# Gate projections of a hybrid layer, started ahead of the recurrence

## The chip, the cores and the metric

The kernel runs on one core of a Trainium2 chip. The metric is the device time of one execution in microseconds; the median of three runs is compared. The profile is of one more execution.

## The reference, cut to what matters

Two layers work on 256 context rows and 1024 latent rows of width 1024. Each layer norms and modulates the rows to h, projects h, runs three branches (gated linear attention, grouped-query attention, an RWKV-7 recurrence) and merges them:

```python
g1, g2, g3 = split(h @ w_in[:, MERGE], 3)              # merge gates, 3 x 1024 columns
m = (sigmoid(g1) * (ya @ w_o_gla) + sigmoid(g2) * (yb @ w_o_att)
     + sigmoid(g3) * (yc @ w_o_rwkv))
x = x + gate * rms_norm(m @ w_out, g_post)
```

The recurrence of the RWKV branch is a scan over time, forwards and backwards:

```python
sa = einsum('bhvk,bhk->bhv', s, kk_t)
s = s * w_t - sa * (kk_t * a_t) + v_t * k_t
y_t = einsum('bhvk,bhk->bhv', s, r_t)
```

The merge gates need only h. They are needed at the merge, after all branches. The last layer needs no gates for the context rows.

## The kernel before

All tokens are in blocks of 256 (context), 512 and 512 columns (`BLK`); tiles have 128 tokens. A product of full accuracy is three matmuls: each operand is split into a high and a low part (`split`, one ACT copy and one DVE subtraction), and high x high, high x low and low x high are summed in PSUM.

A layer has these stages: projections, gated linear attention woven with the attention's projections, the RWKV projections (`rwkv_proj`), then two stages that the change touches, and the merge.

*Attention with the operands.* `rwkv_pre()` makes the operands of the recurrence (decay, key and value factors in `uscr`, the output's factors `gR` and `bR`), block by block and in four groups of 128 rows, and stores them in DRAM. It works on ACT, DVE and POOL and needs little of TensorE; its sums go to the "a" banks of PSUM. `attention()` runs beside it as filler: scores in "mm" banks, transposes in "t", outputs in "o" and "u".

*The pass.* `rwkv()` runs the recurrence: 20 half-steps `q` of 64 tokens in both directions at once. For each, `elem` loads operands and makes AR and BK, `gram` makes products of them and sends a triangular block through DRAM twice (Ms to nscr, back as Lm, 15 steps of DVE, acc to tscr, back as DT and Dg), `merge` builds T from that, and `chain` advances the state S. `merge_gates()` runs beside it as filler: for each block and each of 24 column tiles it loads two times 256 KB of weights (wr), splits them, does 24 matmuls (8 steps of three), and stores the tanh of half the sum to `tg` in DRAM. It begins with the last block, whose normed rows are still in SBUF as `hb[-1]`.

What sets the order: `weave(main, fill, ratio)` takes a step of the main generator, adds `ratio` times its stated length to a debt, and takes steps of the filler until the debt is paid. Steps yield their length: a gate step n / 784, an attention piece n / 256. The program order that comes out is then reordered by the framework's planner (`schedule_with_timeline_sim=True`): for each engine it picks by program order among what it estimates to be ready, and fixes one instruction order for each engine before the run. In the pass the filler has `lead=(0, 8)`: a filler matmul may not be placed before the last matmul of the main step eight steps back. All DMAs are issued on one queue, SP's.

Memory is in pools that open and close like a stack from both sides of SBUF. A new tile waits for the old tiles at its address. On the right, the pool of `merge_gates` comes where `qpool`, the pool of `rwkv_pre`, was. On the left, the pools of the recurrence (`rpool`, `rlate`) come where attention's `bpool` was. `banks(...)` sets which PSUM banks `dense()` hands out in turn: "a", "a" from the RWKV projections' end until the pass, then "mm", "mm", "o". There are two "a" banks.

Of the kernel before, what the change touches and what calls it, by code (L numbers as in the profile page):

```python
# [9 lines left out]
F32 = mybir.dt.float32  # L10
F32R = mybir.dt.float32r
AF = mybir.ActivationFunctionType
# [5 lines left out]
D = 1024  # L18
# [5 lines left out]
BLK = [(0, 256), (256, 512), (768, 512)]  # L24
LAT = [(256, 512), (768, 512)]
GLA0, ATT0, RW0, MG0 = 0, 1568, 3104, 5408
# [44 lines left out]
def hybrid_kernel(ctx: ExitStack, tc: tile.TileContext, I: dict, C: dict, out: bass.AP):  # L71
    nc = tc.nc
    dma = nc.sync.dma_start
    act = nc.scalar.activation
# [18 lines left out]
    pe = PE  # L93

    def nm(s):
        cnt[0] += 1
        return f"{s}{cnt[0]}"
# [3 lines left out]
    def popen(**kw):  # L101
        g = tc.tile_pool(bufs=1, reuse_waits="tile", **kw)
        open_pools.append(g)
        return g, g.__enter__()

    def pclose(g):
        open_pools.remove(g)
        g.__exit__(None, None, None)
# [8 lines left out]
    def ps(tag):  # L117
        return psp.tile([128, 512], F32, tag=tag, bufs=PSB[tag], name=nm("ps_" + tag))
# [3 lines left out]
    def banks(*tags):  # L122

        ring["tags"], ring["i"] = tags, 0

    def dense():
        ring["i"] += 1
        return ps(ring["tags"][(ring["i"] - 1) % len(ring["tags"])])
# [18 lines left out]
    for j in range(2):  # L147
        vec.tensor_scalar(
            out=sil[:, :, j, :], in0=cth[:, j, :].unsqueeze(2).to_broadcast([128, 8, 16]),
# [11 lines left out]
    def dt(name, shape):  # L161
        return dram.tile(shape, F32, name=name)

    yT = {b: dt("yT" + b, [512, NT]) for b in ("att", "gla", "rwkv")}
    tg = [dt(f"tg{i}", [D, NT]) for i in range(3)]
# [4 lines left out]
    xs, hscr = dt("xs", [NT, D]), dt("hscr", [D, NT])  # L170
# [32 lines left out]
    def weave(main, fill, ratio, lead=None, hp=None, to_end=True):  # L203


        due, marks = 0.0, []
        while True:
            with tc.high_priority(offset=hp) if hp else nullcontext():
                w = next(main, None)
            if w is None:  # L210
                break
            marks.append(PE.last.ins)
            due += ratio * (w or 0.0)
            while due > 0.0:
                with tc.issue_after(marks[-1 - lead[1]]) if lead is not None and len(marks) > lead[0] + lead[1] else nullcontext():
                    due -= next(fill, due) or 0.0
        if to_end:
            for _ in fill:
                pass
# [75 lines left out]
    def block_of(b):  # L295

        last = b == len(BLK) - 1
        return [(hX if last else hm).tile([128, 2, BLK[b][1]], F32R, tag=f"b{b}k{k}", name=nm("h")) for k in range(8)]

    def blocks_of(blocks):  # L300
        return [block_of(b) if BLK[b] in blocks else None for b in range(len(BLK))]
# [7 lines left out]
    hb = blocks_of(BLK)  # L309
# [29 lines left out]
    for l in range(DEPTH):  # L339
        need_ctx = l < DEPTH - 1  # L340
        blks = BLK if need_ctx else LAT
# [5 lines left out]
        def split(src, hi, lo):  # L347
            act(out=hi, in_=src, func=AF.Copy)  # L348
            vec.tensor_tensor(out=lo, in0=src, in1=hi.bitcast(F32), op=ALU.subtract)  # L349
# [71 lines left out]
        if l + 1 < DEPTH:  # L421
            mpool, mp = popen(name=nm("modp"))
            md, _ = modulation(l + 1, mp, 2)
# [83 lines left out]
        gpool, gp_ = popen(name=nm("gp"))  # L507
# [324 lines left out]
        def attention():  # L832
# [11 lines left out]
            for g in range(2):  # L844
                kH, kL, V = load(g)
                for t in tiles:
# [56 lines left out]
                    act(out=yo, in_=po[:, :256], func=AF.Copy, scale=0.5)  # L903
                    dma(out=yT["att"][256 * g:256 * g + 256, 128 * t:128 * t + 128].rearrange("(h p) n -> p h n", p=128), in_=yo.rearrange("p (h n) -> p h n", h=2))

        banks("mm", "mm")
        rw = rwkv_proj()
        for _ in range(6):
# [4 lines left out]
        att = attention()  # L913
# [2 lines left out]
        pclose(tpool)  # L916
        pclose(wpool)
        pclose(hpool)
        qpool, qp = popen(name=nm("qp"), side="right")
        weave(rwkv_pre(), att, 4.4)  # L920
        pclose(qpool)
        pclose(bpool)
        rpool, rp = popen(name=nm("rp"))
        def rload(key, shape, src=None):
            t_ = rp.tile(shape, F32, name=nm(key))
            dma(out=t_, in_=C[key] if src is None else src)
            return t_
# [273 lines left out]
        def rwkv():  # L1201
            nq = 2 * NTILE
            es, os = {}, {}

            def put(d, key, steps):
                d[key] = yield from steps

            for w in spread([
                (put(es, 0, elem(0)), 0.0, 0.2, 3.6 + 4 * 2.0),
                (put(os, 0, gram(0, es, 0)), 0.25, 0.5, 5.0 + 6 * 2.0),  # L1210
                (put(os, 1, gram(1, es, 0)), 0.4, 0.65, 5.0 + 6 * 2.0),
                (put(es, 1, elem(1)), 0.6, 0.8, 3.6 + 4 * 2.0),
                (merge(os, 0), 0.75, 1.0, 3.3 + 4 * 2.0),
            ]):
                yield 2.5 * w
            for q in range(nq):
                ths = [(chain(q, os.pop(q)), 0.0, 1.0, 8.3 + 6 * 2.0 + 8 * 2.0 if q % 2 else 8.3 + 6 * 2.0)]
                if q + 1 < nq:
                    ths.append((merge(os, q + 1), *((0.4, 0.9), (0.65, 1.0))[q % 2], 3.3 + 4 * 2.0))
                if q + 2 < nq:  # L1220
                    ths.append((put(os, q + 2, gram(q + 2, es, (q + 2) // 2)), *((0.55, 0.9), (0.1, 0.5))[q % 2], 5.0 + 6 * 2.0))
                if q % 2 == 0 and q // 2 + 1 < NTILE and q:
                    ths.append((put(es, q // 2 + 1, elem(q // 2 + 1)), *(0.0, 0.45), 3.6 + 4 * 2.0))
                yield from spread(ths)


        def merge_gates():
            gpool, gp_ = popen(name=nm("tg"), side="right")
            for t0, n in blks[-1:] + blks[:-1]:
                if (t0, n) == BLK[-1]:  # L1230
                    hx = hb[-1]
                else:
                    hx = block_of(len(BLK) - 1)
                    for k in range(8):
                        raw = gp_.tile([128, 512], F32, tag="wr", bufs=4, name=nm("wr"))[:, :n]
                        dma(out=raw, in_=hscr[128 * k:128 * k + 128, t0:t0 + n])
                        split(raw, hx[k][:, 0, :n], hx[k][:, 1, :n])
                    yield 4.0
                for i in range(3):
                    for m in range(8):  # L1240
                        wh = gp_.tile([128, 8, 128], F32R, tag="wh", bufs=2, name=nm("wh"))
                        wl = gp_.tile([128, 8, 128], F32R, tag="wl", bufs=2, name=nm("wl"))
                        c0 = MG0 + D * i + 128 * m
                        for k in range(0, 8, 4):
                            raw = gp_.tile([128, 512], F32, tag="wr", bufs=4, name=nm("wr")).rearrange("p (k m) -> p k m", k=4)
                            dma(out=raw, in_=I["w_in"][l, 128 * k:128 * k + 512, c0:c0 + 128].rearrange("(k p) m -> p k m", p=128))
                            split(raw, wh[:, k:k + 4], wl[:, k:k + 4])
                        p = dense()[:, :n]
                        for k in range(8):
                            pe.matmul(p, wh[:, k], hx[k][:, 0, :n], start=k == 0, stop=False)  # L1250
                            pe.matmul(p, wh[:, k], hx[k][:, 1, :n], start=False, stop=False)
                            pe.matmul(p, wl[:, k], hx[k][:, 0, :n], start=False, stop=k == 7)
                            if k < 7:
                                yield n / 784
                        th = gp_.tile([128, 512], F32, tag="th", bufs=2, name=nm("th"))[:, :n]
                        act(out=th, in_=p, func=AF.Tanh, scale=0.5)
                        dma(out=tg[i][128 * m:128 * m + 128, t0:t0 + n], in_=th)
                        yield n / 784
            pclose(gpool)

        banks("mm", "mm", "o")
        with tc.manual_schedule(engines={nc.tensor.engine}) if False else nullcontext():
            weave(rwkv(), merge_gates(), (0.76, 0.63)[l], (0, 8), None)
        pclose(rlate)
        pclose(ypool)
        pclose(rpool)
# [27 lines left out]
        for bi, wo in enumerate(("w_o_gla", "w_o_att", "w_o_rwkv")):  # L1294
            if bi == 2:
                mb = blocks_of(blks)
            for jj in range(4):
                wh, wl = load_w([I[wo][l, :, 256 * jj:256 * jj + 256]], kt=4)
                for j in range(2):
                    kr = 2 * jj + j  # L1300
                    w = slice(128 * j, 128 * j + 128)
                    for (t0, n) in blks:
                        th = ta.tile([128, 512], F32, tag="th", bufs=4, name=nm("th"))[:, :n]
                        dma(out=th, in_=tg[bi][128 * kr:128 * kr + 128, t0:t0 + n])
                        p = dense()[:, :n]
# [8 lines left out]
                        m = M[jj][:, j, t0:t0 + n]  # L1314
# [11 lines left out]
        for k in range(8):  # L1326
            wt = cp.tile([128, 2, D], F32R, tag="M", bufs=4, name=nm("wo")) if k < 4 else w2.tile([128, 2, D], F32R, name=nm("wo"))
            for g in range(2):
                gc = slice(512 * g, 512 * g + 512)
                if k < 4:  # L1330
                    raw = cp.tile([128, 512], F32, tag="ws", bufs=2, name=nm("ws"))
                else:
                    if g == 0:
                        xr = oo.tile([128, D], F32, tag="x", bufs=5, name=nm("xr"))
                    raw = xr[:, gc]
# [18 lines left out]
        hb = [None] * len(BLK)  # L1354
# [66 lines left out]
```

## Time and profile before

| | |
|---|---|
| median of 3 runs | 3962.02 us (3959.33 to 3962.11) |
| the profiled execution | 3955.01 us |
| its span, first to last instruction | 3953.2 us |
| mean granted clock of TensorE | 0.962 of full |
| matmuls on TensorE | 31928 |

PE is TensorE's matmuls, PEld its weight loads, DVE VectorE, ACT ScalarE, POOL GpSimd, SPq the queue of SyncE that issues the DMAs. Times in the views count from the span's start. In layer 0 attention with the operands lies at 900 to 1106 us and the pass at 1130 to 1860; in layer 1 at 2900 to 3091 and 3091 to 3720.

### The profile page before, as it was taken

How to read it: one execution, taken by the hardware profiler on the slowest of the kernel's cores; microseconds unless marked ns; L12 is line 12 of the kernel's file. 1: busy time of each engine (PE TensorE's matmuls, PEld its weight loads, DVE VectorE, ACT ScalarE, POOL GpSimd, SP SyncE). 2: the span in 40 equal slices, each digit the busy share in tenths (PEclk: the TensorE clock that was granted, in tenths of full speed). 3: DMA queues.
4: the chain of work that ended last, by engine and by line, in shares of the span. 5: the costliest groups of instructions: out<-in, count | busy, mean ns of one | idle time of the engine just before them, and what ended most of it. 6: DMA issues, size and time to landing. Idle time of an engine off the chain costs nothing.

```text
span 3953.2 us, 81725 instructions
## 1 busy us (share of the span) xinstructions
PE 3698.9 (94%) x31928; PEld 3092.6 (78%) x31928; DVE 2100.1 (53%) x5083; ACT 1761.0 (45%) x4099; POOL 604.9 (15%) x714
## 2 busy tenths in 40 slices
PE   4999999999979989999999999999999899999899
PEld 2799887887767778777888899877878677777687
DVE  3234344437865766664453244444378676666562
ACT  3244437437843444344234344365388333343422
POOL 1133230001200000000233142300022000000042
PEclk7999999999989999999999999999999899999999
DMA  7723222426786777755644232224376676675653
GB/s 221 254 59 88 58 77 96 141 72 186 243 210 138 167 178 178 168 136 162 182 147 137 75 88 79 67 81 128 97 245 202 166 167 162 147 176 119 175 165 116
DMA packets 870964, 568.53 MB, mean 144 GB/s; under 512 B 307568, under 2 KB 775344, under 8 KB 868528
## 3 DMA queue, kind: packets, MB, share of 16 engines
q1 hardware_dynamic: 870576, 563.29, 51.7%
q8 instruction: 251, 4.11, 0.4%
q14 instruction: 137, 1.12, 0.1%
HBM read 379.86 MB, written 183.26 MB: 142 GB/s over the span
## 4 chain that ended last, share of the span: by engine, by line
PE 63%; DMA 14%; DVE 9%; ACT 7%; issue 4%; SPq 2%; POOL 0%; POOLq 0%; DVEq 0%; ACTq 0%
PE ps_mm L85 25%; PE ps_a L85 17%; PE ps_o L85 11%; PE ps_u L85 5%; PE ps_t L85 3%; DMA nscr<-Ms 2%; PE ps_t L90 2%; DMA Lm<-nscr 2%; DMA wr<-in_w_in_dram 1%; DMA tscr<-acc 1%; ACT L158 1%; DMA DT<-tscr 1%; DVE acc L1042 1%; DVE mt L1039 1%; DVE wl L349 1%
## 5 line engine op out<-in xcount | busy, mean ns | idle before, releaser
L85 PE MATMUL ps_mm<-h,wh 128*128 128x512 f32 (+1 forms) x2496 | 759.1, 386 | 14.8 <-DVE rk L683 6.7
L85 PEld LDWEIGHTS ps_mm<-h,wh 128*128 128x128 f32 x2496 | 448.6, 194 | 107.1 <-DVE rk L683 7.8
L349 DVE TENSOR_TENSOR wl<-wr,wh 128x512 fp32r<-128x512 f32 (+1 forms) x464 | 326.9, 726 | 293.1 <-ACT wh L348 287.8
L85 PE MATMUL ps_mm<-h,wl 128*128 128x512 f32 (+1 forms) x1248 | 471.0, 378 | 0.7 <-DVE wl L349 0.7
L348 ACT ACTIVATE wh<-wr 128x512 fp32r<-128x512 f32 (+1 forms) x464 | 271.9, 620 | 394.4 <-PE ps_mm L85 131.2
L85 PE MATMUL ps_mm<-wh,h 128*128 128x256 f32 x2032 | 403.5, 291 | 11.7 <-ACT wh L348 5.6
L85 PEld LDWEIGHTS ps_mm<-wh,h 128*128 128x128 f32 x2032 | 329.1, 195 | 27.3 <-issue 9.8
L85 PE MATMUL ps_a<-h,wh 128*128 128x512 f32 (+1 forms) x1024 | 297.6, 372 | 5.7 <-DVE rk L683 3.6
L85 PE MATMUL ps_mm<-wl,h 128*128 128x256 f32 x1016 | 294.1, 290 | 0.9 <-DVE wl L349 0.9
L85 PE MATMUL ps_o<-h,wh 128*128 128x512 f32 (+1 forms) x928 | 284.9, 388 | 1.1 <-DVE M L1315 1.0
L85 PEld LDWEIGHTS ps_mm<-h,wl 128*128 128x128 f32 x1248 | 241.4, 193 | 47.2 <-issue 4.2
L85 PEld LDWEIGHTS ps_a<-h,wh 128*128 128x128 f32 x1024 | 184.9, 191 | 37.7 <-DVE rk L683 4.4
L85 PEld LDWEIGHTS ps_mm<-wl,h 128*128 128x128 f32 x1016 | 197.6, 195 | 7.8 <-issue 4.9
L85 PE MATMUL ps_o<-wh,h 128*128 128x256 f32 x976 | 197.1, 289 | 2.5 <-ACT h L289 1.2
L1071 POOL COPY T<-Dg 128x512 f32<-128x512 f32 x40 | 28.5, 712 | 1087.8 <-DMA Dg<-dscr 842.4
L85 PEld LDWEIGHTS ps_o<-h,wh 128*128 128x128 f32 x928 | 165.2, 194 | 35.1 <-issue 2.2
L85 PE MATMUL ps_a<-h,wl 128*128 128x512 f32 (+1 forms) x512 | 190.9, 373 | 0.0
L1039 DVE TENSOR_TENSOR mt<-Lm,acc 64x15 f32<-64x15 f32 (+2 forms) x600 | 120.1, 200 | 118.6 <-DMA Lm<-nscr 93.9
L85 PE MATMUL ps_o<-h,wl 128*128 128x512 f32 (+1 forms) x464 | 174.6, 376 | 1.2 <-DVE wl L349 1.2
L85 PEld LDWEIGHTS ps_o<-wh,h 128*128 128x128 f32 x976 | 158.4, 192 | 8.9 <-issue 4.3
L85 PE MATMUL ps_t<-AR,BK 64*128 64x128 f32 x1280 | 127.7, 301 | 25.4 <-DVE BK L992 14.4
L85 PEld LDWEIGHTS ps_t<-AR,BK 64*128 64x128 f32 x1280 | 102.5, 196 | 56.9 <-issue 39.5
(341 smaller groups left out, 7847.6 us busy)
## 6 DMA issues: line engine op xcount, KB each, us to landing
wr<-in_w_in_dram SPq DMA_DIRECT2D x376, 256.0 KB, 3.9
tg<-th SPq DMA_DIRECT2D x96, 256.0 KB, 3.9
th<-tg SPq DMA_DIRECT2D x96, 256.0 KB, 3.0
wm<-in_w_mod_dram SPq DMA_DIRECT2D x16, 1024.0 KB, 7.1
ld_kk<-rscr_kk SPq DMA_DIRECT2D x40, 256.0 KB, 5.0
ld_dc<-rscr_dc SPq DMA_DIRECT2D x40, 256.0 KB, 4.7
ld_ka<-rscr_ka SPq DMA_DIRECT2D x40, 256.0 KB, 5.4
ld_kd<-rscr_kd SPq DMA_DIRECT2D x40, 256.0 KB, 5.4
```

What stands on the lines that cost most here:

```text
L85: PE.last = nc.tensor.matmul(*a, **k)
L90: PE.last = nc.tensor.transpose(*a, **k)
L158: act(out=dst, in_=src, func=AF.Ln, scale=scale, bias=bias)
L348: act(out=hi, in_=src, func=AF.Copy)
L349: vec.tensor_tensor(out=lo, in0=src, in1=hi.bitcast(F32), op=ALU.subtract)
L1039: vec.tensor_tensor(out=mt[:, :n, :w], in0=Lm[:, j, j + 1:16].unsqueeze(2).to_broadcast([64, n, w]), in1=acc[:, j:j + 1, :w].to_broadcast( ...
L1042: vec.tensor_tensor(out=acc[:, j + 1:16, :w], in0=acc[:, j + 1:16, :w], in1=mt[:, :n, :w], op=ALU.add)
L1071: pool.tensor_copy(out=T.rearrange("p d m t -> p (d m t)"), in_=Dg.rearrange("p d m t -> p (d m t)"))
```

## The change

The generator `merge_gates` moves up in the text unchanged, is opened before the operands' pool, follows attention as filler of `rwkv_pre`, and has 12 steps of its own before the pools of the recurrence open. Because it is opened first, its pool lies under `qpool` and stays open through the pass. The filler of `rwkv_pre` has the ratio 5.4 instead of 4.4, that of the pass 0.66 and 0.54 (layers 0 and 1) instead of 0.76 and 0.63. The first gate tiles take their banks from "a", "a".

```diff
+        def merge_gates():
...
         pclose(hpool)
+        gates = merge_gates()
+        next(gates)
         qpool, qp = popen(name=nm("qp"), side="right")
-        weave(rwkv_pre(), att, 4.4)
+
+        def att_gates():
+            for g in (att, gates):
+                for w in g:
+                    yield w
+
+        fill = att_gates()
+        weave(rwkv_pre(), fill, 5.4, to_end=False)
+        for _ in att:
+            pass
         pclose(qpool)
         pclose(bpool)
+        banks("mm", "mm", "o")
+        for _ in range(12):
+            next(gates)
         rpool, rp = popen(name=nm("rp"))
...
-        def merge_gates():
...
         banks("mm", "mm", "o")
         with tc.manual_schedule(engines={nc.tensor.engine}) if False else nullcontext():
-            weave(rwkv(), merge_gates(), (0.76, 0.63)[l], (0, 8), None)
+            weave(rwkv(), gates, (0.66, 0.54)[l], (0, 8), None)
```

## Rows read from the trace of the kernel before

**Rows 1.** The page, part 1: busy time, share of the span, instructions.

```profile
PE 3698.9 (94%) x31928; PEld 3092.6 (78%) x31928; DVE 2100.1 (53%) x5083; ACT 1761.0 (45%) x4099; POOL 604.9 (15%) x714
```

**Rows 2.** Windows: length, busy us (instructions) by engine, PE clock, DMA share, GB/s.

```profile
900.00:1106.00 206.00, 188.45 (x1309) 165.25 (x1307) 170.05 (x481) 174.50 (x460) 41.54 (x50) 0.99 0.70 219
1106.00:1130.00 24.00, 3.82 (x22) 2.52 (x20) 18.97 (x38) 9.43 (x16) 2.98 (x3) 0.59 0.81 236
1130.00:1200.00 70.00, 65.62 (x466) 52.13 (x466) 35.65 (x103) 23.51 (x47) 0.97 (x2) 0.95 0.84 196
1200.00:1860.00 660.00, 615.41 (x8415) 499.51 (x8410) 409.34 (x1076) 275.92 (x552) 25.78 (x28) 0.94 0.68 159
2900.00:3064.00 164.00, 154.03 (x1049) 134.46 (x1049) 137.34 (x378) 142.56 (x365) 38.25 (x46) 0.99 0.73 235
3064.00:3091.00 27.00, 27.00 (x142) 22.78 (x141) 12.60 (x28) 10.18 (x22) 0.92 (x2) 1.00 0.55 148
3091.00:3165.00 74.00, 58.24 (x480) 45.82 (x478) 52.81 (x150) 24.62 (x51) 1.23 (x2) 0.82 0.75 174
3165.00:3720.00 555.00, 518.30 (x7507) 407.01 (x7505) 353.81 (x971) 219.75 (x441) 23.72 (x25) 0.96 0.66 151
```

**Rows 3.** PE's timeline at layer 0's change of stage: start, length, instruction, idle before.

```profile
1113.07 0.80 PE L85 MATMUL ps_a<-sl,ob 128*128 128x512 f32 x1
1128.27 2.08 PE L85 MATMUL ps_t<-AR,BK 64*128 64x128 f32 x16 [14.40 <-DVE BK L992]
...
1132.58 1.05 PE L85 MATMUL ps_mm<-h,wh 128*128 128x512 f32 x2
```

**Rows 4.** PE's timeline in the pass's opening: one gate step of three matmuls.

```profile
1163.40 0.61 PE L85 MATMUL ps_mm<-h,wh 128*128 128x512 f32 x2
1163.86 0.39 PE L85 MATMUL ps_mm<-h,wl 128*128 128x512 f32 x1
1164.08 0.61 PE L85 MATMUL ps_mm<-h,wh 128*128 128x512 f32 x2
```

**Rows 5.** SP's queue at both layers' change of stage.

```profile
1120.12 0.33 SPq L827 DMA_DIRECT2D gR<-th  x1
...
1122.36 3.64 SPq L1246 DMA_DIRECT2D wr<-in_w_in_dram  x4
...
3081.00 0.37 SPq L1246 DMA_DIRECT2D wr<-in_w_in_dram  x1
...
3085.32 0.46 SPq L926 DMA_DIRECT2D smask<-const_smask_dram  x1
```

**Rows 6.** Windows, matmuls of the tile h alone: those of the gates.

```profile
3064.00:3092.00 28.00, 24.30 (x99) 17.99 (x99) 0.00 (x0) 0.00 (x0) 0.00 (x0) 1.00 0.55 152
```

**Rows 7.** PE's timeline in layer 1's opening.

```profile
3142.38 1.95 PE L85 MATMUL ps_u<-DT,G 64*64 64x48 f32 x32 [5.32 <-DMA DT<-tscr]
3144.26 1.22 PE L85 MATMUL ps_mm<-h,wh 128*128 128x512 f32 x2
```

**Rows 8.** PE's waits in layer 0's pass, 1200 to 1860: us, times, longest.

```profile
PE ps_u L85 <- DMA DT<-tscr: 7.2, 5, 2.7
PE ps_u L85 <- DVE T L1088: 6.8, 7, 3.7
PE ps_u L85 <- DVE T L1086: 6.4, 2, 5.7
```

**Rows 9.** Groups by line, layer 0's pass: a gate tile's conversions and tanh.

```profile
L349 DVE TENSOR_TENSOR wl<-wr,wh 128x512 fp32r<-128x512 f32 x128 | 87.2, 702 | 35.0 <-ACT wh L348 30.6 <-ACT Ms L1020 2.8 <-PE ps_mm L85 1.1
L348 ACT ACTIVATE wh<-wr 128x512 fp32r<-128x512 f32 x128 | 74.5, 623 | 78.9 <-PE ps_mm L85 37.8 <-DMA wr<-in_w_in_dram 22.1 <-PE ps_o L85 14.4
L1256 ACT ACTIVATE th<-ps_mm 128x512 f32<-128x512 f32 x26 | 15.1, 580 | 4.4 <-PE ps_mm L85 4.4
```

**Rows 10.** Groups by line on ACT, 900 to 1860.

```profile
L792 ACT ACTIVATE z<-ps_a,prm 128x512 f32<-128x512 f32 (+1 forms) x48 | 29.6, 627 | 4.6 <-PE ps_a L85 4.6
L158 ACT ACT_TABLE_LOAD x10 | 12.8, 1283 | 0.2
```

**Rows 11.** Line L1246, loads of gate weights, 1100 to 1200.

```profile
DMA to landing us min/median/max: 2.9/5.2/8.0
```

## What I expect, before the run

> **What bounds the kernel now.** I read the page's engine shares first, then the span in windows of 5 and 50 us, then PE's timeline, the SP queue and the PE waits around the two places that the change touches. TensorE is busy for 3698.9 us, 94% of the span [rows 1], so the kernel's time is PE's work plus PE's idle time plus what a low clock adds. The change removes no matmul. It can gain only by filling idle PE time, and lose only by making more of it.
>
> The stage windows say where that idle time is [rows 2]. In layer 0, attention with the RWKV operands (900 to 1106) leaves 206 - 188.5 = 17.5 us idle; VectorE and ScalarE are busy for 170 and 174.5 us of it, so three engines are close to full. Then comes a hole: from 1106 to 1130 PE works 3.8 us of 24, so 20.2 us are idle. The opening of the recurrence (1130 to 1200) leaves 4.4 us, and the pass itself (1200 to 1860) 44.6 us in 20 half-steps of 33 us. In layer 1 the same four stretches leave 10.0, 0, 15.8 and 36.7 us: there is no hole there, since gate matmuls already run while attention ends (99 of them, 33 groups of three, between 3064 and 3092 [rows 6]).
>
> The reader should see why layer 0 has a hole and layer 1 has none. In layer 0 PE's last matmul of the operands is at 1113.1 and the next one, the first gram product, at 1128.3, after 14.4 us of waiting for BK [rows 3]. The first weights for a gate are asked for at 1122.4, after the last operand's store of gR at 1120.1 [rows 5]: the gates' pool lies where the operands' pool lay, so it must wait for it. In layer 1 the operands were done earlier than attention, and weights are asked for at 3081, before the recurrence's first constant at 3085.3 [rows 5]. The hole is a wait for memory and for order, not for data: the gates need only the normed block `hb[-1]`, there since the layer began.
>
> **The change, part by part.** *Moved work.* I counted the generators' steps. A step is three 128x512 matmuls; it takes 0.68 us at full clock (1163.40 to 1164.08 [rows 4]). In layer 0 the fill takes 147 units of attention and then 48 gate steps before the operands end (5.4 a unit instead of 4.4); with the one step at the opening and the 12 after, 61 steps or 61 x 0.68 = 41.5 us leave the pass. In layer 1 it is 1 + 59 + 12 = 72 steps, 49 us, of which 33 groups already ran ahead, so about 39 steps or 26.5 us are new. That makes 68 us moved, from the passes to the stages ahead. I sum what becomes of the idle time.
>
> *The hole of layer 0.* With its pool under the operands' pool the gates no longer wait for it. Between the last operand's sum and the first gram product there now stand 12 steps and, by the weave's ratio 0.66 over the first 9 units, some 9 more: 21 x 0.68 = 14.3 us, against 14.4 us of wait. The 6.7 us without work earlier in the hole lie beside the last operand units, which now carry 8 gate steps each. Bounds: nothing filled, or all 20.2 us. I take 16: weights must still arrive (5.2 us median from issue to landing [rows 11], two tiles ahead, 5.5 us of PE work in each), so some edge stays.
>
> *The clock.* [...] Work from 1128.3 to 1133.9 at half speed loses 2.8 us. I take 2.5 gained; bounds 0 and 3. [...]
>
> *The stages before.* Moving 7.6 and 9 tiles brings their conversions along: two ACT copies of 0.62 us, two DVE subtractions of 0.70 and a tanh of 0.58 a tile [rows 9], so 14 us of ScalarE and 11 us of VectorE in layer 0, in a stage that grows by 41.5 us of PE. They lie beside that PE work; without this cover they would cost up to 14 us. Tanh brings no table load: none stands at its line, only at lines such as L158 [rows 10]. The first gate tile takes one of the two "a" banks and keeps it until its last matmul, which is written behind attention; the operands then share the other. The tanh of the operands waits 4.6 us in all for those sums today, over 48 sums [rows 10]. A sum with its tanh, 0.63 us and two matmuls, needs some 1.5 us, and 60 of them 90 us of 206. So I cost it at nothing, with 10 us as the bound. Each tile also puts two loads and a store on the SP queue, where the operands' loads and stores stand behind a load that waits for a buffer; some 24 issues of 0.4 to 0.5 us in 230 us are small. Gates that are ready fill some of the 17.5 + 10 us idle: I take 4, bounds 12 gained and 10 lost.
>
> *Layer 1's opening.* Of the 15.8 us only part can be filled: at 3142.4 PE stands 5.3 us before a recurrence matmul that waits for a DMA round trip [rows 7], and gate matmuls stand behind it in the queue. I take 4 of 15.8; bounds 0 and 12.
>
> *The passes.* With 0.66 for 0.76 and 0.54 for 0.63 a half-step gets some 13% fewer gate steps and ends about 2 us earlier, so the recurrence's latencies have less to hide behind. The waits there are many and short: 7.2 us for DT, 6.8 and 6.4 us for T in layer 0 [rows 8]. I let the idle 44.6 + 36.7 us grow by 9 (some 11%); this holds the end of layer 1, where my count has the gates run out about 8 units before the pass ends. Bounds: no growth, or half of the 68 us not given back, 34.
>
> Sum: -16 - 2.5 - 4 - 4 + 9 = -17.5 us. The profiled execution took 3955.0 us, of which the span is 3953.2; with the sum it is 3937.5. The median of the runs, 3962.0, lies 7.0 above the profiled one, so I forecast 3945 us.
>
> **The rivals.** *All of it is filled* (the gates flow through both openings and the passes keep their idle time): -20 - 3 - 10 - 8 = -41, so 3921. For it: layer 1 shows gate matmuls filling attention's tail with PE at 27.0 of 27 us [rows 2]. Against it: DMA is busy 0.84 of 1130 to 1200 already [rows 2], and weights come through the same engines.
>
> *The filler stands in the wrong place in the queue.* PE's order is fixed before the run by estimated times; a gate matmul behind a recurrence matmul that waits covers nothing, as at 3142.4 [rows 7]. Then only the 12 steps written ahead count, 8.2 us, and with the passes' growth of 9 the time is 3963, no change. [...] Against this rival: the hole in layer 0 lies ahead of the first gram product, where the new steps are written first.
>
> *The passes do not give back what left them*, the rival on the other side. Place: the chain from Ms through two DMA round trips to the merge, whose product waits for DT 5 times in layer 0's pass today [rows 8]. If that chain, not PE, sets the half-step, the step does not shorten when gates leave it. It decides when more than 26.5 of the 68 us moved stay behind as idle time. At 60%, 41 us, the time is 41 - 26.5 = 14.5 us above 3962, so 3977. For it: every half-step has such waits. Against it: they are 44.6 of 660 us now, so PE sets the step in 93% of it.
>
> **How the numbers follow.** Forecast, 3937 to 3954: 0.35. All filled, below 3937: 0.22. Wrong place, 3954 to 3970: 0.19. Passes not shorter, above 3970: 0.24. A measurement of this kernel tells about 0.2%, 7.9 us, from no change. The first two are faster by more than that, 0.57; the third is the same, 0.19; the last slower, 0.24. The range leaves a tenth out at either side: 3920 takes in nearly all of the second, 3980 the worked case of the last; the likeliest case's own range is 3937 to 3954.
>
> **What would show it.** Right: no PE hole ahead of layer 0's first gram product and a clock that stays at full there; gate matmuls on "a" banks in the operands' stage; wr loads before the last gR store; each pass shorter by most of 41 and 26 us, with waits of about the same sum. Wrong: PE idle for over 10 us before the first gram product with gate matmuls behind it; the waits for DT, T and ET much above those of rows 8; the operands' tanh waiting long for its bank; or half-steps still at 33 us.

## The result, and the profile after

The changed kernel takes 4003.29 us (median of 4 runs, 3999.58 to 4008.70); the kernel before takes 3961.77 on the same chip. The ratio is 1.0112 [1.0098, 1.0127]: slower by 1.1%, against a forecast of 3945 us and a range of 3920 to 3980. The profiled execution took 4001.22 us with a span of 3999.4, 46.2 above the span before. (The medians are 41.5 apart: the profiled execution of the kernel before was 7 us under its median, this one 2 under.)

TensorE has the same matmuls and is busy 13 us longer; the other 33 us are idle time [rows 1]:

```profile
PE 3712.3 (93%) x31928; PEld 3111.7 (78%) x31928; DVE 2107.0 (53%) x5083; ACT 1762.9 (44%) x4099; POOL 606.3 (15%) x714
```

I cut each layer at three marks: attention's first output store, the first gram product (the *stage* with attention and operands lies between them), and the merge's first load of attention's output (up to it is the *pass*). The 46.2 us are then: +6.4 before layer 0's stage, +2.1 in layer 0 (29.0 - 26.9), -0.6 between, +35.9 in layer 1 (48.9 - 13.0), +2.4 behind. Windows of the kernel after (columns as in [rows 2]): layer 0's stage and pass, then layer 1's.

```profile
921.10:1163.70 242.60, 226.03 (x1445) 195.91 (x1443) 184.07 (x498) 184.10 (x461) 44.16 (x52) 0.99 0.72 218
1163.70:1882.30 718.60, 650.21 (x8703) 527.96 (x8703) 442.85 (x1176) 287.02 (x578) 27.80 (x30) 0.92 0.68 160
2822.50:3150.70 328.20, 306.10 (x1820) 265.79 (x1820) 213.15 (x546) 212.43 (x512) 42.38 (x54) 0.98 0.59 181
3150.70:3775.20 624.50, 550.98 (x7796) 433.10 (x7797) 399.93 (x1102) 236.02 (x474) 26.91 (x28) 0.90 0.63 146
```

The same stretches of the kernel before:

```profile
914.70:1128.30 213.60, 178.36 (x1229) 155.71 (x1227) 173.67 (x479) 170.13 (x438) 44.07 (x52) 0.95 0.71 220
1128.30:1873.80 745.50, 696.17 (x8943) 564.51 (x8944) 454.56 (x1197) 304.88 (x608) 28.14 (x30) 0.94 0.70 164
2814.60:3093.90 279.30, 263.01 (x1618) 225.94 (x1617) 197.94 (x527) 196.46 (x488) 42.65 (x54) 0.99 0.59 187
3093.90:3731.40 637.50, 585.89 (x8010) 458.95 (x8010) 412.63 (x1125) 249.67 (x499) 27.29 (x28) 0.94 0.67 154
```

Take the first two numbers of each row. In layer 0 the stage's idle time falls from 35.2 to 16.6 us, the pass's rises from 49.3 to 68.4: what one gains the other loses. In layer 1 the stage had little idle time to fill (16.3, after 22.1), and the pass's rises from 51.6 to 73.5, at a clock of 0.90 instead of 0.94.

The forecast's first step came true. The stretch that held the hole [rows 2] is full and at full clock (1.00), and up to the first gram product, from 1130 to 1163.7, PE is busy for 33.2 of 33.7 us; that product stands behind gate products (ps_o) with no wait [rows 3]; and the gates' weights are asked for long before the operands' last store [rows 5]. One window of all engines, PE's timeline, and SP's queue:

```profile
1106.00:1130.00 24.00, 24.00 (x151) 21.29 (x149) 13.18 (x34) 12.48 (x28) 2.84 (x5) 1.00 0.47 141
```

```profile
1163.13 0.61 PE L85 MATMUL ps_o<-h,wh 128*128 128x512 f32 x2
1163.68 1.16 PE L85 MATMUL ps_t<-AR,BK 64*128 64x128 f32 x16
```

```profile
1100.79 0.38 SPq L926 DMA_DIRECT2D wr<-in_w_in_dram  x1
...
1157.23 0.45 SPq L827 DMA_DIRECT2D gR<-th  x1
```

How much work moved, by the matmuls that read the tile h (PE alone; length, busy us (count), clock, DMA share, GB/s): layer 0's stage after, then layer 1's stage before and after.

```profile
921.10:1163.70 242.60, 52.84 (x218) 0.99 0.72 218
```

```profile
2814.60:3093.90 279.30, 76.59 (x317) 0.99 0.59 187
```

```profile
2822.50:3150.70 328.20, 125.48 (x521) 0.98 0.59 181
```

218 matmuls are 73 steps of three, at 0.68 us [rows 4] 49.6 us; layer 1 has 204 more, 68 steps or 46.2 us. (The forecast had 61 and 39. It left out of this count the 9 steps that it has itself ahead of the first gram product; where layer 1's other 20 come from is open.) The layer 0 stage grew by 29.0 us for 49.6 of work, so 20.6 us were filled; layer 1's by 48.9 for 46.2, so nothing was. The passes gave back 26.9 and 13.0 of these 95.8 us.

Where does the pass's new idle time lie? The forecast named the waits for DT and T [rows 8]. T is written in three rounds, the first by an addition (L1086, after the change L1135), the others by a copy (L1088, after L1137), and all have to be counted. PE's waits for T on VectorE, in layer 0's pass before and after:

```profile
PE ps_u L85 <- DVE T L1086: 9.5, 3, 5.7
...
PE ps_u L85 <- DVE T L1088: 6.8, 7, 3.7
PE ps_a L85 <- DVE T L1088: 4.9, 2, 2.8
```

```profile
PE ps_u L85 <- DVE T L1137: 20.0, 9, 7.5
...
PE ps_u L85 <- DVE T L1135: 1.8, 4, 0.6
...
PE ps_a L85 <- DVE T L1137: 0.2, 1, 0.2
```

And in layer 1's pass before and after:

```profile
PE ps_u L85 <- DVE T L1086: 10.0, 3, 5.1
...
PE ps_u L85 <- DVE T L1088: 2.5, 5, 0.9
...
PE ps_a L85 <- DVE T L1088: 2.1, 2, 1.1
```

```profile
PE ps_u L85 <- DVE T L1137: 24.7, 8, 9.3
...
PE ps_u L85 <- DVE T L1135: 7.9, 5, 2.8
...
PE ps_a L85 <- DVE T L1137: 1.2, 1, 1.2
```

The wait for DT is where it was (7.2 and 6.8 us in layer 0, 12.6 and 12.6 in layer 1). That for T goes from 14.6 to 33.8 us in layer 1, which is most of the 21.9 us more idle time there. In layer 0 it does not grow (21.2 and 22.0): the 19 us there are spread over many small waits. Layer 1's longest one shows what is ahead of T on VectorE (timeline of DVE and PE):

```profile
3620.23 0.18 DVE L1088 TENSOR_TENSOR mt<-Lm,acc 64x15 f32<-64x15 f32 x1 [7.96 <-DMA Lm<-nscr]
...
3623.99 0.42 DVE L1137 COPY T<-ps_u 32x256 f32<-32x256 f32 x1
3624.46 0.61 PE L85 MATMUL ps_u<-T,ET 64*16 64x16 f32 x32 [9.35 <-DVE T L1137]
```

VectorE stands 8 us before the next half-step's triangular block, which comes back from DRAM as Lm; the copy into T, for the half-step that PE works on, is queued behind it, and PE waits 9.4 us for it.

### The profile page after: what moved, and what is told of

Read it like the earlier page. It is cut to its first block, busy times and chain, and to the rows that moved or that the text cites. A ratio compares the mean times of both kernels' runs of the same rounds, so it can differ in the third digit from the quotient of the medians.

```text
span 3999.4 us, 81727 instructions
## 1 busy us (share of the span) xinstructions
PE 3712.3 (93%) x31928; PEld 3111.7 (78%) x31928; DVE 2107.0 (53%) x5083; ACT 1762.9 (44%) x4099; POOL 606.3 (15%) x714
## 4 chain that ended last, share of the span: by engine, by line
PE 63%; DMA 14%; DVE 10%; ACT 7%; issue 3%; SPq 2%; POOL 0%; DVEq 0%; POOLq 0%; ACTq 0%
PE ps_mm L85 24%; PE ps_a L85 19%; PE ps_o L85 10%; PE ps_u L85 5%; PE ps_t L85 3%; PE ps_t L90 2%; DMA nscr<-Ms 2%; DMA Lm<-nscr 2%; DVE mt L1088 2%; DMA wr<-in_w_in_dram 1%; DVE acc L1091 1%; ACT L158 1%; DMA tscr<-acc 1%; DVE wl L349 1%; ACT L159 1%
## 5 line engine op out<-in xcount | busy, mean ns | idle before, releaser
L85 PE MATMUL ps_mm<-h,wh 128*128 128x512 f32 (+1 forms) x2352 | 715.9, 387 | 19.2 <-DVE rk L683 8.0
L85 PEld LDWEIGHTS ps_mm<-h,wh 128*128 128x128 f32 x2352 | 425.9, 196 | 106.3 <-DVE rk L683 9.1
L349 DVE TENSOR_TENSOR wl<-wr,wh 128x512 fp32r<-128x512 f32 (+1 forms) x464 | 326.9, 724 | 279.3 <-ACT wh L348 277.3
L85 PE MATMUL ps_mm<-h,wl 128*128 128x512 f32 (+1 forms) x1176 | 444.7, 378 | 0.1
L85 PE MATMUL ps_a<-h,wh 128*128 128x512 f32 (+1 forms) x1264 | 373.5, 377 | 5.2 <-DVE rk L683 3.5
L85 PEld LDWEIGHTS ps_a<-h,wh 128*128 128x128 f32 x1264 | 229.8, 191 | 46.5 <-DVE rk L683 4.4
L85 PE MATMUL ps_o<-h,wh 128*128 128x512 f32 (+1 forms) x832 | 251.8, 385 | 3.1 <-DVE M L1329 3.1
L85 PE MATMUL ps_a<-h,wl 128*128 128x512 f32 (+1 forms) x632 | 238.0, 377 | 0.0
L1088 DVE TENSOR_TENSOR mt<-Lm,acc 64x15 f32<-64x15 f32 (+2 forms) x600 | 122.3, 204 | 115.1 <-DMA Lm<-nscr 95.7
L85 PEld LDWEIGHTS ps_o<-h,wh 128*128 128x128 f32 x832 | 146.0, 193 | 32.4 <-DVE M L1329 2.4
L85 PEld LDWEIGHTS ps_o<-wh,h 128*128 128x128 f32 x976 | 157.9, 192 | 10.8 <-issue 4.3
L85 PE MATMUL ps_o<-h,wl 128*128 128x512 f32 (+1 forms) x416 | 154.6, 372 | 0.9 <-DVE wl L349 0.9
L898 POOL TENSOR_TENSOR y<-y,sg 128x128 f32<-128x128 f32 x64 | 37.0, 578 | 767.7 <-DVE y L897 649.1
L871 DVE TENSOR_REDUCE mx<-ps_mm 128x1 f32<-128x512 f32 (+1 forms) x200 | 117.5, 590 | 55.5 <-PE ps_mm L85 53.9
```

The source lines that it names most:

```text
L85: PE.last = nc.tensor.matmul(*a, **k)
L871: vec.tensor_reduce(out=mx[:, i:i + 1], in_=s[:, :n], axis=AX.X, op=ALU.max, negate=True)
L898: pool.tensor_tensor(out=y[:, hc], in0=y[:, hc], in1=sg[:, hc], op=ALU.mult)
L1088: vec.tensor_tensor(out=mt[:, :n, :w], in0=Lm[:, j, j + 1:16].unsqueeze(2).to_broadcast([64, n, w]), in1=acc[:, j:j + 1, :w].to_broadcast( ...
```

## The experiments

Two theories, as they are lettered in the expectations. **A**, the third rival: a half-step has a length of its own, set by the recurrence's chain with its round trips through DRAM, so gates taken out of the pass leave idle time. **B**: any edit makes the planner deal out a new instruction order for all that follows, and the kernel before has a lucky deal (a *deal* is one such order, a *draw* one profiled execution of it). Some expectations also name a third possibility, that PE's work alone sets the time. Each ratio below is to the kernel before on the same chip, with its 95% interval.

**Nothing moved (n1_null, n12_null2, j4_before).** Only the pass's ratio is touched, by a hundredth or less.

```diff
-            weave(rwkv(), merge_gates(), (0.76, 0.63)[l], (0, 8), None)
+            weave(rwkv(), merge_gates(), (0.75, 0.62)[l], (0, 8), None)
```

n12_null2 has (0.77, 0.64) and j4_before (0.765, 0.635).

> Kernel before with the pass's fill ratios 0.75 and 0.62 instead of 0.76 and 0.63; nothing is moved. Theory A (a gate step taken out of the pass frees only some 40% of its PE time, because the half-step also has a latency of its own) expects 3962 within 6 us. Theory B (the planner deals the order anew at any edit, and the kernel after drew a bad one) expects a move of 15 us or more, of either sign.

> Kernel before with the ratios 0.77 and 0.64, nothing moved; with n1_null it sizes what a new order alone does. Theory A with a small re-dealing: within 12 us of before. Theory B: 15 us or more away, of either sign.

> Kernel before with the ratios 0.765 and 0.635, nothing moved. If the kernel before had a lucky draw, 8 to 30 us above it, like the two at 0.01 from its ratios (23 and 25 us above). If those two were unlucky, within 8 us of it.

Measured: 1.0064 [1.0043, 1.0085], 1.0058 [1.0044, 1.0073], 1.0059 [1.0019, 1.0100]. Three edits that move no work cost about 24 us each, where A had allowed 6 and 12. That is half of what the change costs, and speaks for B. (They do touch both passes' ratios, so the filler is spaced anew in both.)

**The change with a slightly different text (j1_after, j2_after, j3_after).** Ratios of the pass (0.67, 0.55), (0.65, 0.53), and 13 opening steps instead of 12:

```diff
-        for _ in range(12):
+        for _ in range(13):
             next(gates)
```

> Kernel after with the pass's ratios 0.67 and 0.55. If the move itself costs layer 1, its stages from the first attention store to the merge take 940 to 955 us again, as in the kernel after (953) and n5_dense (942), against a mean of 930 for unmoved layers. If the draw was the cause, they scatter from 915 to 950 like those.

> Kernel after with the pass's ratios 0.65 and 0.53. As for j1_after: 940 to 955 us for layer 1's stages if the move costs, 915 to 950 if the draw does. Layer 0's stages at some 960 us either way, since its pass is thin.

> Kernel after with 13 opening steps for 12. As for j1_after: 940 to 955 us for layer 1's stages if the move costs, 915 to 950 if the draw does.

Measured: 1.0106 [1.0072, 1.0140], 1.0033 [1.0013, 1.0053], 1.0112 [1.0080, 1.0143]. With the change itself: four deals, mean 1.0091, from 1.0033 to 1.0112. The three null edits have a mean of 1.0060. The change's own part is then nearer to 0.3% than to 1.1%. In layer 1, j1 and j3 came as a cost of the move has it (944.5 and 951.1 us); j2 did not (931.3, and 939.7 instead of some 960 in layer 0).

**The pool alone (n2_pool).** `merge_gates` opens its pool ahead of the operands' pool (it yields once before its first tile) and stays out of attention's filler; all ratios are the old ones.

```diff
+            gpool, gp_ = popen(name=nm("tg"), side="right")
+            yield 0.0
...
+        gates = merge_gates()
+        next(gates)
```

> The gates' pool opens ahead of the operands' pool, as in the kernel after, but no gate step is written ahead: attention alone fills the operands at 4.4, and the pass has its old ratios 0.76 and 0.63. Theory A: the pass keeps its filler and gives nothing away, while layer 0's hole of 20 us can be filled from the pass's first steps, so 3942 to 3958. Theory B: anywhere from 3930 to 4000. Theory C (the gates' pool and first bank hurt the operands' stage) expects 3965 or more.

Measured: 0.9984 [0.9968, 1.0000]. In the window that held the hole PE is now busy throughout. But the hole has only moved: just ahead of the first gram product, 15 us later than before, PE works 1.7 of 13.1 us, and that product waits 11.4 us for BK where it waited 14.4 [rows 3]. Two windows, and PE's timeline:

```profile
1106.00:1130.00 24.00, 24.00 (x124) 20.31 (x123) 14.11 (x25) 12.01 (x22) 3.49 (x4) 1.00 0.72 227
1130.00:1143.10 13.10, 1.70 (x9) 1.11 (x7) 12.06 (x25) 6.40 (x11) 0.00 (x0) 0.73 1.01 291
```

```profile
1143.10 2.08 PE L85 MATMUL ps_t<-AR,BK 64*128 64x128 f32 x16 [11.40 <-DVE BK L1039]
```

So the place of the pool lets 120 gate matmuls (40 steps) run in this stage, and does not close the hole; in the changed kernel, which has the steps written ahead as well, it is closed. Layer 0's stage and pass take 952.6 us together for 959.1. It is the fastest kernel measured here that does all the work, and not clearly faster than the one before.

**Layer 0 alone (n4_layer0, n5_dense, n9_l0_dense, n10_l0_denser, v1_l0, v2_l0).** n4 makes the change in layer 0 and leaves layer 1's text as it was, with the ratios (0.66, 0.63). n9, n10, v1 and v2 are n4 with 0.76, 0.86, 0.74 and 0.78 for 0.66, that is, layer 0 moved but its pass about as dense as before, or denser. n5 is the change in both layers with the old ratios (0.76, 0.63).

```diff
+        if l == 0:
+            gates = merge_gates()
+            next(gates)
...
+        if l == 0:
+            weave(rwkv_pre(), fill, 5.4, to_end=False)
+        else:
+            weave(rwkv_pre(), att, 4.4)
...
+            weave(rwkv(), gates, (0.66, 0.63)[l], (0, 8), None)
```

> The change in layer 0 alone; layer 1 as in the kernel before. Theory A, from the two traces: layer 0 lost 8.5 us, so 3970 within 6. Theory B: layer 0 keeps its 8 us lost, and layer 1, dealt anew, lands anywhere within 20 us of that.

> Kernel after with the pass's old ratios 0.76 and 0.63: the pass is as dense as before until its gates run out some three half-steps early. Theory A (the half-step has a latency floor, most of all in layer 1): the dense part gives back nothing and the starved end runs at the floor, so between the kernels, some 15 us above before. If thin filling was the harm, layer 1's pass returns most of its 46 us and the total is at most 5 us above before.

> The change in layer 0 alone, with the pass's old ratio 0.76 there; layer 1 as before. From the trace of n5_dense, whose layer 0 took 936 us from the first attention store to the merge against 959 before: theory A expects 20 to 25 us under before. If that was a lucky order, within 8 us of before.

> As n9_l0_dense with the ratio 0.86 in layer 0's pass. Theory A: the dense steps stay bound by PE and the gates run out earlier, at a floor of some 30 us a half-step; no better than n9_l0_dense, 0 to 15 us above it. If only density mattered, 5 us or more under it.

> The change in layer 0 alone with the ratio 0.74 in its pass, layer 1 as before. If filler spacing is the cause, layer 0's stages take 930 to 942 us again (before 959, with 0.66 940 to 961). Layer 1 draws from 916 to 945, so the total is 24 us under before to 10 above.

> As v1_l0 with 0.78 in layer 0's pass. Layer 0's stages 930 to 945 us; the total again by layer 1's draw, 24 us under before to 10 above.

Measured: n4 1.0015 [1.0000, 1.0030], n5 1.0030 [1.0013, 1.0046], n9 1.0042 [1.0029, 1.0055], n10 1.0064 [1.0048, 1.0080], v1 1.0040 [1.0026, 1.0054], v2 1.0047 [1.0028, 1.0066]. In layer 0, stage and pass together, the dense versions take 931.6 to 952.7 us (n9, v1, n5, n10, v2: mean 941), the thin ones 939.7 to 961.2 (j2, j1, j3, n4, after: mean 953.5), the unmoved ones 950.0 to 959.1 (null2, n1, j4, before: mean 955.8).

So with the old ratio kept the move seems worth some 15 us there, with a spread between the kernels as large as that. At layer 1's first mark 8 us of it are left (means of 2803.1 us for the dense and 2811.2 for the unmoved), since these kernels also reach layer 0's stage 4 us later and lose 2 behind the pass. Against the kernel before none of it reached the total; against the null kernels (mean 1.0060) the four with layer 0 alone moved and dense (mean 1.0048) are 0.1% faster.

The expectations of n4 and n10 (9 us above n9) held, and so did v1's for layer 0; n9's totals (20 to 25 us under before, or within 8; it is 17.6 above), v2's layer 0 and the totals of v1 and v2 (12 and 16 above) missed, and n5 fell between its two.

The reason why the gain does not show lies in a stage that the kernels with layer 0 alone don't touch. The middle of layer 1's pass (first to last product with DT; n4, v1, the second null kernel), same text, same matmuls but a few records:

```profile
3143.80:3683.70 539.90, 510.43 (x7293) 399.68 (x7293) 359.63 (x1002) 212.88 (x433) 22.42 (x26) 0.95 0.67 153
```

```profile
3126.90:3704.40 577.50, 530.79 (x7301) 414.40 (x7301) 360.85 (x1004) 214.34 (x435) 22.40 (x26) 0.91 0.63 143
```

```profile
3141.50:3711.00 569.50, 526.75 (x7309) 411.37 (x7308) 357.16 (x1002) 214.86 (x435) 22.26 (x26) 0.93 0.63 144
```

n4 and v1 differ only in layer 0's ratio, and layer 1 takes 38 us longer in v1: 17 us more idle, 20 us more busy at a lower clock. The order does differ there. With like matmuls in a row as one group, 1074 of the 1183 groups of n4's pass in layer 1 stand in the same order in v1's trace; n4 and the kernel before have 1140 in common. But not all of the 38 us is the deal. In that pass v1, v2, n9 and n10 share 1159 or more of some 1180 groups, and still it takes 650.8 to 670.7 us: a profile is one execution. v1's took 3973.5 us, and the median of its ten runs is 3962.3. The order shows better from group to group: the kernel before and n4 have a mean of 635 us, these four 659.

All the draws of layer 1, from the profiled executions (stage and pass in us):

| kernels | layer 1 | stage | pass | sum |
|---|---|---|---|---|
| before | unmoved | 279.3 | 637.5 | 916.8 |
| n1, null2, j4 | unmoved | 282 to 284 | 643.7, 661.1, 656.6 | 927.2, 945.0, 938.5 |
| n2, n4, n9 | unmoved | 283 to 286 | 634.4, 632.7, 660.0 | 920.4, 915.8, 943.7 |
| n10, v1, v2 | unmoved | 282 to 283 | 655.4, 670.7, 650.8 | 937.3, 953.3, 932.6 |
| after | moved | 328.2 | 624.5 | 952.7 |
| n5, j1 | moved | 325.0, 324.2 | 617.4, 620.3 | 942.4, 944.5 |
| j2, j3 | moved | 325.5, 327.8 | 605.8, 623.3 | 931.3, 951.1 |

Ten unmoved draws have a mean of 933.1 and a standard deviation of 13 us; the kernel before is one of the two best of them. (They are not ten deals: two sets among them, of two and of four, share most of their order.) Five moved ones have a mean of 944.4. Moving layer 1's gates costs 11 us on the mean, with a standard error of 5 or 6 by the spreads, so it is barely clear of nothing: 43 us more in the stage, 32 less in the pass. The +35.9 of the two profiles is that 11 plus a draw that was 16 us better than the mean before and 8 worse after.

**Work taken out (n3_drop, n6_floor).** If PE set the step, less PE work would shorten it. n3 is the kernel before with the new ratios, and leaves out three of a gate tile's eight steps in as many tiles as make 60 steps in layer 0 and 72 in layer 1, 90 us; n6 leaves out six of eight steps everywhere, 443 us, at a quarter of the ratios. Loads, splits and tanh all stay.

```diff
-                        for k in range(8):
+                        for k in (0, 7):
...
-            weave(rwkv(), merge_gates(), (0.76, 0.63)[l], (0, 8), None)
+            weave(rwkv(), merge_gates(), (0.19, 0.1575)[l], (0, 8), None)
```

> Kernel before without the PE work of 60 gate steps in layer 0 and 72 in layer 1 (three of the eight matmul groups are left out in 20 and 24 tiles of the last block, so those gates are not the reference's), loads and conversions kept, and the ratios 0.66 and 0.54. 132 steps of 0.684 us are 90 us. If PE alone set the pass, 3872. Theory A: 40% come back, 3926. Under 20% would be 3944 or more.

> Kernel before with two of the eight matmul groups of every gate tile (so the gates are not the reference's), loads and conversions kept, ratios 0.19 and 0.1575. PE loses 443 us of work. If PE set the passes, 3962 - 443 = 3519. Theory A: layer 1's pass, 637 us from its first gram product to the merge, stays above 580, layer 0's falls from 745 to some 650, and the total is 3800 or more.

Measured: n3 0.9960 [0.9943, 0.9976], 17 us faster for 90 us of work; n6 0.9858 [0.9828, 0.9888], 58 us faster for 443. Measured from the null kernels it is some 40 and 80. For n3 that is 20% or 45% of the work, where PE alone would give all of it and A 40%. The passes of n6:

```profile
1129.90:1833.30 703.40, 529.37 (x7654) 430.14 (x7655) 454.04 (x1198) 302.31 (x609) 29.82 (x30) 0.75 0.72 175
3043.40:3670.30 626.90, 469.13 (x7220) 385.54 (x7221) 406.48 (x1121) 246.94 (x498) 28.78 (x28) 0.76 0.65 154
```

With a quarter of the filler the passes are 42 and 11 us shorter. The idle time goes from 49 and 52 us to 174 and 158, and the clock from 0.94 to 0.75. So with little filler PE's work does not set the pass's length: that half of A holds. The 94% of [rows 1] hid it, since the filler is what fills. But 700 and 625 us are no floor: j2, which only moves gate work ahead and leaves none out, has passes of 697.7 and 605.8. The end of a pass, where the filler drains, blurs the comparison. From the first gram product to the last product with DT, layer 0 takes, before, after and in n6:

```profile
1128.30:1816.80 688.50, 645.43 (x8402) 523.90 (x8402) 431.32 (x1157) 281.69 (x570) 25.48 (x28) 0.94 0.71 165
1163.70:1824.90 661.20, 600.22 (x8162) 487.86 (x8161) 419.56 (x1136) 263.80 (x540) 25.14 (x28) 0.92 0.70 161
1129.90:1779.90 650.00, 485.49 (x7209) 397.15 (x7211) 427.21 (x1152) 272.39 (x558) 25.90 (x27) 0.74 0.72 171
```

These stretches hold 1635, 1394 and 384 matmuls on h: the first 241 fewer make it 27 us shorter, the next 1010 only 11. In layer 1 the same stretch takes 591.5, 591.6 and 585.9 us with 987, 843 and 231. What does set it is not shown, and n6 is no clean measure of the recurrence's chain. It still loads every gate weight, and these loads are the largest item, 10.8%, of the chain of work that ended last in layer 0's pass; and at the clock of 0.74 the matmuls other than the gates' keep PE busy for some 370 us of this stretch, before for 300.

**The thin ratio alone (n11_ratio).** The kernel before with (0.66, 0.54); the gates left over run behind the recurrence.

> Kernel before with the new ratios 0.66 and 0.54 alone; no gate step is written ahead, so those left over run alone after the pass. Theory A: the thin passes are no shorter and the left-over steps add their PE time, 40 to 70 us above before. If PE alone set the passes, within 8 us of before.

Measured: 1.0058 [1.0041, 1.0076], the same as the null kernels; the 40 to 70 us that A expected are not there. Layer 0's pass, the thin part and the drain:

```profile
1126.20:1781.60 655.40, 600.49 (x8219) 490.72 (x8220) 419.67 (x1142) 269.08 (x546) 26.82 (x28) 0.94 0.70 165
1781.60:1873.40 91.80, 90.02 (x732) 73.26 (x729) 33.50 (x56) 36.88 (x63) 2.98 (x3) 1.00 0.55 163
```

The thin part has 54.9 us of idle time in 655; before, the whole pass had 49.3 in 745. The drain then runs with 1.8 idle, at full clock (1.00), and the total of both is that of before (747.2 for 745.5). A thin pass alone is not what costs 40 us, and A in the strong form of that expectation fell. The thin part ends with the last product with DT and holds 1452 matmuls on h: for 183 fewer than before, some 42 us, it is 33 us shorter. So down to there most of the work comes back; the change has 58 fewer still, and its stretch (661.2 us) is no shorter.

**The round trips cut (n7_after_cut, n8_before_cut).** Lm, DT and Dg are read from a slot that an earlier half-step wrote, so that no half-step waits for its own data to come back; the recurrence's values change, its instructions stay.

```diff
-            dma(out=Lm, in_=diag(ns))
+            dma(out=Lm, in_=diag(nscr[(q + 1) % NSCR]))
...
-            dma(out=DT.rearrange("p h d m t -> p (h d m) t"), in_=full(ts))
+            dma(out=DT.rearrange("p h d m t -> p (h d m) t"), in_=full(tscr[(q + 1) % NSCR]))
```

> Kernel after, with each half-step reading Lm, DT and Dg from the DRAM buffers of an earlier half-step, so that nothing in it waits for its own two DMA round trips; the inverse is then not its own, and the result not the reference's. Theory A with the round trip as the floor: 40 us or more faster than the kernel after, and within 15 us of the kernel before with the same cut. If the floor is the state's own chain of products, it gains under 15 us.

> Kernel before with the same cut (Lm, DT and Dg of an earlier half-step). Theory A with the round trip as the floor: 10 to 30 us faster than before, since the denser pass hides most of the trip already. If the round trip does not matter, within 8 us of before.

Measured: n7 1.0050 [1.0034, 1.0067], n8 1.0099 [1.0076, 1.0123]. n8 was to be 10 to 30 us faster and is 38 slower than the kernel before, 15 slower than the null kernels. The change alone, read between the two, is a gain of 0.5% with this edit in both. Layer 1's pass, n7 and then n8:

```profile
3148.70:3739.00 590.30, 536.02 (x7795) 419.91 (x7796) 393.17 (x1102) 235.92 (x474) 27.11 (x28) 0.94 0.65 153
```

```profile
3107.00:3756.30 649.30, 595.89 (x8009) 463.87 (x8010) 405.66 (x1122) 249.19 (x498) 25.03 (x28) 0.93 0.64 150
```

It takes 590.3 us in n7, less than in any of the five moved draws (605.8 to 624.5), with 54.3 us idle and a clock of 0.94 where the change had 73.5 and 0.90. In n8 it takes 649.3, inside the unmoved draws, and layer 0 shows nothing (718.3 in n7, 718.6 after). n7 is 24 us faster than the change by the ratios, between the 40 and the 15 of its expectation.

But the edit does not take the trips out of a half-step's way. acc and mt have one buffer each (accT takes that of mt), and VectorE's first write into one for the next half-step waits for a store to DRAM: in all 36.7 us for that of acc in the changed kernel, 47.8 for acc and 21.9 for accT in n7. VectorE's two longest waits in layer 1's pass, after and then in n7:

```profile
DVE mt L1088 <- DMA Lm<-nscr: 37.5, 12, 8.0
DVE acc L1078 <- DMA tscr<-acc: 36.7, 15, 5.1
```

```profile
DVE acc L1079 <- DMA tscr<-acc: 47.8, 17, 8.8
DVE mt L1089 <- DMA dscr<-accT: 21.9, 13, 7.0
```

The wait for Lm is gone, and a wait for the store of accT stands in its place: 69.7 us in all for 74.2. In n8 the two are 91.6 for 80.4 before. So the pair is no test of a half-step without round trips, each is one deal, and whether the trips bind stays open.

## Why the prediction was wrong, step by step

- *What bounds the kernel.* "The kernel's time is PE's work plus PE's idle time plus what a low clock adds" holds as a sum. What was made of it, "it can gain only by filling idle PE time", does not say who sets a half-step's length. n6 answers that.
- *The hole, the clock.* -16 and -2.5 forecast, and with the stage's -4 that is 22.5 us; 20.6 were filled. Right for the idle time. Behind the 2.5 stands the clock granted in the kernel before: 0.50 from 1128.27 to 1133.90, with PE busy throughout, after the 0.59 of the window with the hole [rows 2]. In the changed kernel it is 1.00 from 1106 to 1188, but then 0.56 to 1193, with PE idle for 3.6 of these 5 us, and 0.76 to 1198. So no run shows the 2.5 by itself: the opening has its low clock later. The forecast left this out, and also the clock of the passes in n6, 0.75 and 0.76. "The hole is a wait for memory and for order": of the two it was mostly the order, for with the gates' pool out of the way n2 keeps 11.4 of the 14.4 us.
- *No cost on the "a" banks.* Right: the operands' tanh waits 5.7 us for its sums, before 4.6 [rows 10].
- *Layer 1's opening.* -4 forecast, with 39 new steps. From the first gram product to the first with DT 8.5 us are idle, before 10.5, so 2 came. 68 steps moved, and the stage ahead grew by 2.7 us more than the work; over all the draws by 2.8 less (means of 326.1 for five moved and 282.8 for ten unmoved).
- *The passes: the step that failed.* "I let the idle 44.6 + 36.7 us grow by 9." In the two profiles the passes' idle time grew by 41.0 us (19.1 and 21.9), and with the lower clock (0.92 for 0.94 and 0.90 for 0.94) 55.9 of the 95.8 us moved stay behind (22.7 and 33.2). Over all the deals it is some 31 us: the pass gives back 32.5 of 49.6 in layer 0 (means of 710.9 for five thin and 743.4 for four unmoved) and 32.0 of 46.2 in layer 1. Rival three's point was 26.5 us, and on the same means the stages filled 22 (19.4 and 2.8). So the loss is that rival's, and the runs bear out one half of its mechanism, "if that chain, not PE, sets the half-step": in layer 0 PE's work does not set it below some 1450 gate matmuls, and the move goes 58 below that. That the chain through DRAM does is not shown. The argument against the rival, that waits are 44.6 of 660 us, was the error: a wait that the filler covers does not show as a wait (49 us idle in layer 0's pass before, 174 in n6). The sum of waits is no measure of the slack. Its sign of half-steps "still at 33 us" came near: 33.7 us before and 32.4 after in layer 0, 28.6 and 28.8 in layer 1 (19 steps between the first and the last product with DT).
- *What the forecast didn't hold at all.* It summed as if all that the change leaves alone would stay as it is. Three edits that move nothing cost 0.6%. The kernel before is a good deal of a planner; an edit draws a new one. In numbers: mean cost of the move some 0 in layer 0's stage and pass, 11 us in layer 1 and 5 ahead of layer 0's stage; the rest of the 46 is deals and single executions.
- *Before layer 0's stage:* +6.4, not foreseen. All ten kernels with the ratio 5.4 in layer 0 and no cut reach that mark at 916.8 to 921.2 us, those with 4.4 and no cut at 912.7 to 916.8. The means are 919.1 and 914.3, so some 5 us belong to the change; the cause is open.

The likeliest account: about a quarter of the loss is the move, half is the end of a good deal (B, the null kernels' 0.6%), the rest the deal that came instead. That a deal alone costs so much was shown by edits that move nothing; that with less filler PE's work does not set a half-step, by taking work out. The shares are estimates from a few draws each. Open: what does set a half-step (the round trips were not taken out of it, VectorE's order behind Lm was read in the trace and not tried, and the gate weights' loads stay in every kernel here), and why the same matmuls run at a clock of 0.95 in one profile and at 0.91 in another.

## What to carry to other kernels

An engine that is 94% busy with filler is not thereby the bound: take most of the filler out once and look at what the time does, before you pay for moving it. Filler moved ahead is worth what it fills there minus what it covered where it was; here that was 22 us against 31 on the means. Where a planner deals out the order, run two or three edits that move nothing and take their spread as the uncertainty of any change, for repeated runs of one kernel don't show it. And look behind the window in which a hole has closed: it may have moved.

## What was not expected of the hardware

With three quarters of the gate matmuls gone, the granted clock in the passes fell from 0.94 to 0.75 and 0.76, so that part of the work saved came back as slower work: some 370 us for 300 in the other matmuls of layer 0's stretch. In layer 1's middle the change shows a lower clock too, before and after:

```profile
3142.40:3685.40 543.00, 508.60 (x7292) 398.75 (x7292) 359.94 (x1009) 213.09 (x433) 23.35 (x25) 0.95 0.67 152
```

```profile
3195.30:3742.30 547.00, 490.83 (x7161) 385.19 (x7161) 352.77 (x996) 202.10 (x413) 24.68 (x26) 0.91 0.62 140
```

The matmuls on h in these stretches took 260.8 us before and 232.5 after, 28.4 less; PE's busy time fell by only 17.8, for the rest took 10.6 us longer at 0.91. With 21.8 us more idle time, a stretch with 131 fewer matmuls is 4.0 us longer. Here it need not be the filler: v1 has all of it in this stretch, and 0.91 as well. The clock goes with PE's idle time in these stretches, 0.95 with 29 and 34 us (n4, before), 0.93 with 43 (the second null kernel), 0.91 with 47 and 56 (v1, after); which of the two is the cause is not shown.
